# Modulating the first mixer's input in four blocks, and summing three conditioning vectors by scalings and accumulating transfers

## The chip, the core and the metric

The kernel runs on one core of a Trainium2 chip. The core has five instruction queues that run side by side and meet at semaphores: TensorE (PE, with its weight loads shown as PEld), VectorE (DVE), ScalarE (ACT), GpSimd (POOL) and SyncE (SP), which here only starts transfers. Each queue runs in order: an instruction that waits holds up all that stand behind it. The metric is the time of one execution on the device in microseconds (us); less is better.

## The reference

Two layers act on 256 tokens of 1024 features, all in float32. Each layer has a mixer and then a product-key expert block (PEER). The conditioning vector `c` gives six vectors per layer, by which the inputs are shifted and scaled and the outputs gated:

```
sh1, sc1, g1, sh2, sc2, g2 = split(silu_c @ ada_w[i] + ada_b[i], 6)
hx = x * (1 + sc1) + sh1
hc = ctx * (1 + csc1) + csh1                      # layer 0: the context too, from silu(c_ctx)
q, k, v, gu, gv = split(hx @ w_in)                # layer 0; the context gives k and v alone
a = differential attention of q over the keys and values of context and input, head norm
g = gelu(gu) * (w_s . layer_norm(gelu(gv)) + b_s)  # spatial gate
x = layer_norm(alpha * x + g1 * (concat(a, g) @ w_out))
x = layer_norm(alpha * x + g2 * peer(x * (1 + sc2) + sh2))
```

Layer 1 has a pooling mixer in place of attention. The change touches the first mixer only: how `sh1` and `sc1` of layer 0 reach `hx`, and how `g1`, `sh2` and `sc2` of layer 0 are summed.

## The kernel before

**Streaming.** All large weights come as tiles of 128 x 1024 floats (512 KB). A list of items is worked off in order: each item has a source tile and a function with its matmuls. `load` starts the transfer into `raw` (four buffers), on SP's queue, four items ahead; `split` makes of it a high part `hi` on ScalarE (line 64) and a low part `lo` = raw - hi on VectorE (line 68), three items ahead. A product of two float32 matrices is three matmuls of such parts. Every second tile of the opening uses buffers of its own (`xraw`, `xhi`, `xlo`). An item's `after` runs behind its matmuls, and `defer` puts work behind the next item's. All instructions are written out in one order per engine; nothing is moved at run time.

**Opening.** The first 16 items are the shift and scale weights, 8 tiles of 128 input rows each: for each tile, six matmuls with the two columns of `silu(c)` and `silu(c_ctx)` (`cparts`) into two accumulators, one per 512 columns. When a vector's eight tiles are done, ScalarE copies its two rows to SBUF (`adrow`, line 545), TensorE transposes them to columns (line 562), and VectorE adds the bias (line 563). Only with both vectors done does `modulated` (lines 582 to 585) make the modulated input `h` in two halves. Then the items of `w_in` begin: four tiles for `gv` (line 610, two blocks of 128 features each), four for `gu` (line 616), then four head groups of six tiles: two for the keys of input and context, two for the queries, two for the values (line 870). The context `hc` is modulated beside `gu`: ScalarE makes the high parts, GpSimd the full product (line 584), VectorE the difference.

**Head groups.** After the second key tile, `rope` copies the rotated rows on ScalarE (`rp`, line 702); VectorE multiplies and adds (lines 707 to 711) and splits the result. In the first group the exponent of lambda (line 526) and the spatial gate (`sgt`, lines 668 and 669) follow. A pipeline of scores, exponent (`ex`, line 735), transposes and value products is interleaved from there on.

**Three conditioning vectors.** `g1`, `sh2` and `sc2` of layer 0 aren't made by matmuls over `cparts`: `ada` loads eight tiles `aw` per vector, and VectorE adds tile times a column of `csil` into `aacc` (a scaling, line 391, and seven fused additions, line 393). `end` sums over the 128 partitions with matmuls by a column of ones (line 400 for a column vector, line 407 for the row vector `g1`, which goes to memory as `grow`, line 409, on ScalarE's queue). `chained` strings the vectors together; `ada_step` takes one step, and the items of a head group take 2, 2, 1, 1, 1 and 1. `aw` has three buffers, so a load waits for the addition three before it. The same `ada` serves seven vectors in layer 0's expert block.

Of the kernel before, what the change touches and what calls it, by code (L numbers as in the profile page):

```python
# [35 lines left out]
class Build:  # L36
# [335 lines left out]
            self.holds += 1  # L372


    def ada(self, pool, l, j, kind, dst, ahead=1):

        nc = self.nc
        st = {}  # L380

        def load(k):
            w = st["w", k] = pool.tile([128, 1024], FT, name="aw", bufs=3)
            nc.sync.dma_start(w, self.a["ada_w"][l, 128 * k:128 * k + 128, 1024 * j:1024 * j + 1024])

        def step(k):
            w = st.pop(("w", k))
            c = self.csil[:, k, 0:1]
            if k == 0:
                st["acc"] = pool.tile([128, 1024], FT, name="aacc", bufs=1)  # L390
                nc.vector.tensor_scalar(st["acc"], w, c, None, op0=OP.mult)
            else:
                nc.vector.scalar_tensor_tensor(st["acc"], w, c, st["acc"], op0=OP.mult, op1=OP.add)  # L393

        def end():
            acc = st["acc"]
            if kind == "col":
                p = self.pt()
                for k in range(8):
                    nc.tensor.matmul(p[:, k:k + 1], acc[:, 128 * k:128 * k + 128], self.ones[:, 0:1], start=True, stop=True)  # L400
                nc.vector.tensor_add(dst, p[:, :8], self.adabc[:, l, j])
            else:
                w = st["w", 8]
                for c in range(2):
                    s = slice(512 * c, 512 * c + 512)
                    p = self.pt()
                    nc.tensor.matmul(p[0:1], self.ones[:, 0:1], acc[:, s], start=True, stop=True)
                    nc.vector.tensor_add(w[0:1, s], p[0:1], w[0:1, s])
                nc.scalar.dma_start(dst, w[0:1])
        def go(i):  # L410
            if i < 8:
                load(i)
            elif i == 8 and kind == "row":
                w = st["w", 8] = pool.tile([128, 1024], FT, name="aw", bufs=3)
                nc.sync.dma_start(w[0:1], self.a["ada_b"][l:l + 1, 1024 * j:1024 * j + 1024])
            if i >= ahead:
                step(i - ahead)
        return [lambda i=i: go(i) for i in range(8 + ahead)], end

    @staticmethod  # L420
    def chained(vectors):

        q, end = [], None
        for steps, e in vectors:
            for i, s in enumerate(steps):
                q.append([end, s] if i == 1 and end else [s])
            end = e
        q += [[], [], [end]]
        return deque(lambda fs=fs: [f() for f in fs] for fs in q)


# [47 lines left out]
    def first(self):  # L479
# [50 lines left out]
        self.hook(start)  # L530


        for j in range(2):
            for k in range(8):
                def run(hi, lo, j=j, k=k):
                    if k == 0:
                        st["ad"] = [self.pa(), self.px()]
                    for c in range(2):
                        cs = slice(512 * c, 512 * c + 512)
                        self.mm3(st["ad"][c][0:2], (self.cparts[0][:, k], self.cparts[1][:, k]), (hi[:, cs], lo[:, cs]),  # L540
                                 k == 0, k == 7)
                    if k == 7:
                        row = st["G"].tile([2, 1024], FT, name="adrow", bufs=1)
                        for c in range(2):
                            nc.scalar.activation(row[:, 512 * c:512 * c + 512], st["ad"][c][0:2], AF.Copy)
                        if j == 0:
                            self.defer(lambda: self.defer(lambda: self.defer(lambda: columns_of(0, row))))
                        else:
                            columns_of(1, row)
                            nc.vector.tensor_scalar(st["cc"][:, 1], st["cc"][:, 1], 1.0, None, op0=OP.add)  # L550
                            self.release(1)
                            modulated(0)
                            self.ahead(self.now, 1)
                            modulated(1)
                self.item(a["ada_w"][0, 128 * k:128 * k + 128, 1024 * j:1024 * j + 1024], run,
                          after=(lambda q=k: inputs(0, [q])) if (j, k) in ((1, 0), (1, 1)) else None,
                          own=(lambda: st["E"]) if k % 2 else None, owned=2, early=k % 2)

        def columns_of(j, row):
            p = self.pt()  # L560
            for b in range(8):
                nc.tensor.transpose(p[:, 2 * b:2 * b + 2], row[:, 128 * b:128 * b + 128], self.ident[0:2, 0:2])
            nc.vector.tensor_add(st["cc"][:, j], p[:, :16].rearrange("p (k o) -> p k o", o=2),
                                 self.adabc[:, 0, j][:, :, None].to_broadcast([128, 8, 2]))


        self.holds += 1
# [5 lines left out]
        def modulated(q):  # L573
            if q == 0:
                self.hhi, self.hlo = self.htiles()
            x, y = st["in"][q], st["in"][q | 2]
            hi = self.hhi[q] if q < 2 else st["hc"][q - 2]
            lo = self.hlo[q] if q < 2 else st["hc"][q]
            for k in range(4):
                kk, o = 4 * (q % 2) + k, q // 2  # L580
                sc, sh = st["cc"][:, 1, kk, o:o + 1], st["cc"][:, 0, kk, o:o + 1]
                nc.scalar.activation(hi[:, k], x[:, k], AF.Identity, scale=sc, bias=sh)
                eng = nc.gpsimd if q else nc.vector
                eng.tensor_scalar(y[:, k], x[:, k], sc, sh, op0=OP.mult, op1=OP.add)
            nc.vector.tensor_sub(lo, y, hi.bitcast(FT))

        def others():

            P = st["P"]
            st["ada"] = self.chained([self.ada(P, 0, j, *(("row", self.growd[0][0]) if j == 2 else ("col", self.adac[:, 0, j])))  # L590
                                      for j in (2, 3, 4)])

        def ada_step(n=1):
            for _ in range(n):
                f = st["ada"] and st["ada"].popleft()
                if f:
                    f()

        def hc(k, s=slice(0, 256)):
            return st["hc"][k // 4][:, k % 4, s], st["hc"][2 + k // 4][:, k % 4, s]  # L600
# [18 lines left out]
        w = a["w_in"]  # L619
        n = 0  # L620

        for t in range(4):
            def run(hi, lo, t=t):
                if t == 0:
                    st["gv"] = [self.pa(), self.pa()]
# [2 lines left out]
                if t == 3:  # L628
# [19 lines left out]
                    def affine(nb):  # L648
# [23 lines left out]
        for t in range(4):  # L672
# [7 lines left out]
            def after(t=t):  # L680
                if t == 0:
                    small_loads("wsT", "sgu_b")
                if t == 1:
                    small_loads("lam", "ng")
                if t == 3:
                    lams()
                if t in (1, 2):
                    modulated(t + 1)
                if t == 3:
                    pe.close()  # L690
                    others()
                    st["K"] = pt_.enter_context(tc.tile_pool(name="kq", bufs=1))
            self.item(w[n], run, after=after)
            n += 1

# [20 lines left out]
        def scores(g, h, nb):  # L716
# [37 lines left out]
        def mix(g, h):  # L754
# [1 line left out]
            aT = st.pop(("aT", g, h))  # L756
            v = st["v", g]
            if h == 0:
                st["sq"] = T.tile([128, 2, 256], FT, name="sq", bufs=2)
# [139 lines left out]
        def after():  # L899
# [3 lines left out]
            if k == 8:  # L903

                assert not st["ada"]
                *st["res"], st["grow"] = [st["P"].tile([128, 1024], FT, name="aw", bufs=3) for _ in range(3)]
# [540 lines left out]
def _layout(i):  # L1447
# [5 lines left out]
    a = dict(x=g["x"][0], ada_w=g["ada_w"], ada_b=g["ada_b"], ln_g=g["ln_g"], ln_b=g["ln_b"])  # L1453
    for n, x in (("xT", "x"), ("cT", "ctx")):
        a[n] = g[x][0].T.reshape(2, 4, 128, 256).transpose(0, 2, 1, 3).reshape(2, 128, 1024)
    a["cc"] = np.stack([g["c"][0].reshape(8, 128).T, g["c_ctx"].reshape(8, 128).T], axis=2)
    a["ada_bc"] = cols(g["ada_b"].reshape(2, 6, 1024))
    a["ln_gc"], a["ln_bc"] = cols(g["ln_g"]), cols(g["ln_b"])
# [44 lines left out]
```

## Time and profile before

| | us |
|---|---|
| median of 3 runs | 2038.82 |
| lowest, highest | 2037.8, 2040.18 |
| the profiled execution, as a run | 2038.5 |
| its span, first to last instruction | 2036.7 |
| PE, DVE, ACT, POOL busy in the span | 1965.6, 1558.0, 969.6, 289.9 |

The first mixer is the first 260 us or so of the span; the opening ends at 49.50 us, and the output product of the mixer begins at 233.98 us. The profile takes one execution. A matmul's row lasts longer than the step to the next one, since matmuls overlap; the step is read from the starts. In square brackets a row names the idle time of the engine ahead of it and what ended it. Rows of DMA starts on a queue (SPq, ACTq) may last until a buffer came free.

### The profile page before, as it was taken

Reading aid. Unit: us, or ns where it says so; the run is one execution under the profiler, and the core shown is the slowest. Engines: PE = TensorE matmul, PEld = TensorE weight load, DVE = VectorE, ACT = ScalarE, POOL = GpSimd, SP = SyncE. Lnnn points to the kernel's source line nnn. Section 1 sums busy time; section 2 is a strip of 40 time slices with the busy share of each in tenths; the row PEclk is TensorE's granted clock in tenths of the full one; section 3 lists DMA queues with packets and bytes.
Section 4 is the critical chain, followed back from the end, with each engine's and each line's share of the span. In section 5 each row is a group of like instructions: output and inputs, shape, how many; then the busy total and the mean of one; then the engine's idle time right before and its main releaser. Section 6 shows DMA issues by size and latency. Waiting matters only on the chain.

```text
span 2036.7 us, 34041 instructions
## 1 busy us (share of the span) xinstructions
PE 1965.6 (97%) x13348; PEld 1771.4 (87%) x13348; DVE 1558.0 (76%) x2775; ACT 969.6 (48%) x1354; POOL 289.9 (14%) x134
## 2 busy tenths in 40 slices
PE   8899989999999999999999889999999999999997
PEld 4889869999999998888778779999999998888886
DVE  6878878998888757777776679998888655555566
ACT  6444554544544444444445554445544444444442
POOL 0100007891000000000000016890000000000001
PEclk9899999999999999999999989999999999999999
DMA  8534335554444558888877445554444556555663
GB/s 305 216 135 159 132 116 174 177 176 165 157 148 150 170 185 285 291 305 293 288 263 223 144 161 161 182 176 165 156 146 147 177 180 198 191 195 195 219 236 113
DMA packets 108178, 389.93 MB, mean 191 GB/s; under 512 B 12777, under 2 KB 12905, under 8 KB 108017
## 3 DMA queue, kind: packets, MB, share of 16 engines
q1 hardware_dynamic: 105416, 382.28, 55.8%
q10 hardware_dynamic: 2024, 3.38, 0.5%
q8 instruction: 104, 1.70, 0.3%
q0 software_dynamic: 576, 2.10, 0.3%
q14 instruction: 58, 0.47, 0.1%
HBM read 384.55 MB, written 3.16 MB: 190 GB/s over the span
## 4 chain that ended last, share of the span: by engine, by line
PE 66%; DVE 25%; ACT 4%; issue 3%; DMA 2%; ACTq 0%; SPq 0%; DVEq 0%
PE pa L323 26%; PE px L323 8%; PE pa L984 8%; PE pa L985 7%; PE pa L988 7%; PE pt L1136 2%; DVE lo L68 2%; ACT hi L64 2%; PE pa L616 1%; DVE oh L1063 1%; DVE oh L1068 1%; DVE topi L1014 1%; DVE sc L1015 1%; DVE topi L1017 1%; PE pa L870 1%
## 5 line engine op out<-in xcount | busy, mean ns | idle before, releaser
L64 ACT ACTIVATE hi<-raw 128x1024 fp32r<-128x1024 f32 x599 | 632.6, 1059 | 581.5 <-PE px L323 357.0
L68 DVE TENSOR_TENSOR lo<-raw,hi 128x1024 fp32r<-128x1024 f32 x491 | 599.5, 1224 | 368.8 <-ACT hi L64 366.8
L984 PE MATMUL pa<-h,hi 128*128 128x256 f32 x2304 | 577.9, 288 | 1.5 <-DVE h L287 1.3
L985 PE MATMUL pa<-h,hi 128*128 128x256 f32 x2304 | 566.2, 283 | 0.3
L323 PE MATMUL pa<-hi,h 128*128 128x512 f32 x1524 | 471.7, 391 | 3.3 <-ACT h L285 1.6
L984 PEld LDWEIGHTS pa<-h,hi 128*128 128x128 f32 x2304 | 441.8, 192 | 2.5 <-DVE h L287 2.1
L985 PEld LDWEIGHTS pa<-h,hi 128*128 128x128 f32 x2304 | 442.6, 192 | 0.9 <-DVE h L290 0.9
L323 PEld LDWEIGHTS pa<-hi,h 128*128 128x128 f32 x1524 | 286.3, 188 | 65.9 <-ACT h L285 1.8
L988 PE MATMUL pa<-h,lo 128*128 128x256 f32 x2304 | 323.4, 283 | 0.0
L988 PEld LDWEIGHTS pa<-h,lo 128*128 128x128 f32 x2304 | 297.7, 192 | 0.0
L68 POOL TENSOR_TENSOR lo<-raw,hi 128x1024 fp32r<-128x1024 f32 x106 | 271.0, 2575 | 81.9 <-ACT hi L64 81.6
L323 PE MATMUL pa<-lo,h 128*128 128x512 f32 x762 | 256.5, 391 | 0.1
L323 PE MATMUL px<-hi,h 128*128 128x512 f32 x508 | 197.5, 389 | 0.0
L323 PEld LDWEIGHTS pa<-lo,h 128*128 128x128 f32 x762 | 143.8, 189 | 30.6 <-DVE lo L68 0.5
L1150 ACT ACTIVATE A<-pt 128x256 f32<-128x256 f32 (+31 forms) x182 | 50.9, 310 | 229.1 <-DVE A L1148 215.9
L949 POOL DMA_DIRECT2D xhd<-xh x4 | 2.4, 596 | 960.0 <-PE pt L273 949.8
L323 PEld LDWEIGHTS px<-hi,h 128*128 128x128 f32 x508 | 95.3, 188 | 19.8
L1127 DVE TENSOR_TENSOR m<-e,gd 128x512 f16<-128x512 f16 x256 | 105.4, 454 | 2.2
L323 PE MATMUL px<-lo,h 128*128 128x512 f32 x254 | 98.8, 389 | 0.0
L259 POOL TENSOR_TENSOR aw<-aw 128x512 f32<-128x512 f32 x4 | 5.3, 1344 | 644.6 <-ACT aw L254 644.4
L393 DVE SCALAR_TENSOR_TENSOR aacc<-aw,csil,aacc 128x1024 f32<-128x1024 f32 x70 | 89.5, 1279 | 3.5 <-DMA aw<-in_ada_w 3.4
L1136 PE MATMUL pt<-m,e 128*128 128x128 f16 x1024 | 81.7, 220 | 3.2 <-DVE m L1127 1.0
(365 smaller groups left out, 2151.7 us busy)
## 6 DMA issues: line engine op xcount, KB each, us to landing
raw<-in_uT SPq DMA_DIRECT2D x256, 512.0 KB, 3.5
raw<-in_peer_v SPq DMA_DIRECT2D x256, 512.0 KB, 4.1
aw<-in_ada_w SPq DMA_DIRECT2D x80, 512.0 KB, 5.3
raw<-in_w_in SPq DMA_DIRECT2D x32, 512.0 KB, 4.1
raw<-in_wq SPq DMA_DIRECT2D x32, 512.0 KB, 3.8
raw<-in_ab_w_out SPq DMA_DIRECT2D x12, 512.0 KB, 3.5
raw<-in_ada_w SPq DMA_DIRECT2D x8, 512.0 KB, 5.9
xraw<-in_ada_w SPq DMA_DIRECT2D x8, 512.0 KB
```

The lines of the kernel that those rows point to most:

```text
L64: nc.scalar.activation(hi, it["raw"], AF.Copy)
L68: low()
L323: nc.tensor.matmul(acc[2 * nb + a // 512], s[x], w[:, a:b], start=i == 0 and part == 0, stop=i == last and part == 2)
L393: nc.vector.scalar_tensor_tensor(st["acc"], w, c, st["acc"], op0=OP.mult, op1=OP.add)
L616: nc.tensor.matmul(o, (hi, lo)[x][:, 128 * k:128 * k + 128], f(k)[y], start=k == 0 and part == 0, stop=k == 7 and part == 2)
L870: nc.tensor.matmul(p, h(k, s)[x], tiles[k // 4][y][:, 256 * (k % 4):256 * (k % 4) + 256], start=part == 0 and k == 0, stop=part == 2 and k ...
L984: mm(out, hi[:, cs], hh, start=k == 0, stop=False)
L985: mm(out, hi[:, cs], hl, start=False, stop=False)
L988: mm(out, lo[:, cs], self.h(k)[0], start=False, stop=k == 7)
L1127: nc.vector.tensor_tensor(v4(x), v4(st["e1"][:, s]), wide(st["gd"][i], ch, 4), op=OP.mult)
L1136: nc.tensor.matmul(p[:, 128 * j:128 * j + 128], e2[:, j], m[i][:, j], start=i == 0, stop=i == 1)
L1150: nc.scalar.activation(x[:, e:], y[:, e:], AF.Copy, scale=1.0 / 4096)
```

## The change

The opening goes by blocks of 256 columns: `quarter(c)` takes four tiles that hold 256 columns of shift and 256 of scale for all 1024 input rows (a new layout `ada01`), copies one row of 512 to SBUF, transposes it into four column pairs, and `modulated(c)` makes two blocks of 128 features of `h`, all on ScalarE and VectorE. The `gv` tile that reads these two blocks follows one block later: blocks 1 and 2, `w_in` tile 1, block 3, tile 2, block 4, tiles 3 and 4. The context tiles are loaded later (behind the fourth `gv` tile), and `modulated_ctx` makes both products on ScalarE.

`ada` gets a second form for the first mixer's three vectors (`dma`): ScalarE scales each tile, tiles 1 and 2 straight into two sums, the others in place; GpSimd starts a transfer that adds the scaled tile to sum 1 or 2 in turn, and after the eighth tile one that adds sum 2 to sum 1. Steps run two loads behind (`ahead=2`), `aw` has four buffers, two steps are taken before the first head group, and a vector's `end` stands two steps into the next one. To make room, the attention's `ex` buffers go from six to five and `sq` from two to one.

```diff
-    def ada(self, pool, l, j, kind, dst, ahead=1):
+    def ada(self, pool, l, j, kind, dst, ahead=1, dma=False):
...
-            w = st["w", k] = pool.tile([128, 1024], FT, name="aw", bufs=3)
+            w = st["w", k] = pool.tile([128, 1024], FT, name="aw", bufs=4 if dma else 3)
...
         def step(k):
             w = st.pop(("w", k))
             c = self.csil[:, k, 0:1]
+            if dma:
+
+                if k < 2:
+                    st["sum", k] = dma.tile([128, 1024], FT, name=f"aacc{k}", bufs=1)
+                acc = st["sum", k % 2]
+                nc.scalar.activation(w if k > 1 else acc, w, AF.Copy, scale=c)
+                if k > 1:
+                    nc.gpsimd.dma_start(acc, w, accum_op=OP.add)
+                if k == 7:
+                    nc.gpsimd.dma_start(st["sum", 0], acc, accum_op=OP.add)
+                    st["acc"] = st["sum", 0]
+                return
...
-    def chained(vectors):
+    def chained(vectors, at=1):
...
-                q.append([end, s] if i == 1 and end else [s])
+                q.append([end, s] if i == at and end else [s])
             end = e
-        q += [[], [], [end]]
+        q += [[]] * (at + 1) + [[end]]
...
-        for j in range(2):
-            for k in range(8):
-                def run(hi, lo, j=j, k=k):
...
+        def quarter(c):
+            for kk in range(4):
+                def run(hi, lo, kk=kk):
+                    if kk == 0:
+                        st["ad"] = self.px() if c % 2 else self.pa()
+                    for i in range(2):
+                        k, cs = 2 * kk + i, slice(512 * i, 512 * i + 512)
+                        self.mm3(st["ad"][0:2], (self.cparts[0][:, k], self.cparts[1][:, k]), (hi[:, cs], lo[:, cs]), k == 0, k == 7)
+                    if kk < 3:
+                        return
+                    row = st["G"].tile([2, 512], FT, name="adrow", bufs=2)
+                    nc.scalar.activation(row, st["ad"][0:2], AF.Copy)
+
+                    def turned():
+                        columns_of(c, row)
+                        modulated(c)
+                    if c == 3:
+                        self.defer(turned)
+                    else:
+                        self.defer(lambda: self.defer(turned))
...
+        def modulated(c):
...
+            for k in range(2):
+                i, kk = 2 * (c % 2) + k, 2 * c + k
+                sc, sh = st["cc"][:, 1, kk, 0:1], st["cc"][:, 0, kk, 0:1]
+                nc.scalar.activation(hi[:, i], x[:, i], AF.Identity, scale=sc, bias=sh)
+                nc.vector.tensor_scalar(y[:, k], x[:, i], sc, sh, op0=OP.mult, op1=OP.add)
+            nc.vector.tensor_sub(lo[:, ks], y, hi[:, ks].bitcast(FT))
+
+        def modulated_ctx(q):
...
+                nc.scalar.activation(hi[:, i], x[:, i], AF.Identity, scale=sc, bias=sh)
+                nc.scalar.activation(x[:, i], x[:, i], AF.Identity, scale=sc, bias=sh)
+            nc.vector.tensor_sub(lo, x, hi.bitcast(FT))
...
+            st["ada"] = self.chained([self.ada(P, 0, j, *(("row", self.growd[0][0]) if j == 2 else ("col", self.adac[:, 0, j])),
+                                               ahead=2, dma=st["K"]) for j in (2, 3, 4)], 2)
+            ada_step(2)
...
+        quarter(0)
         for t in range(4):
+            if t < 3:
+                quarter(t + 1)
+
             def run(hi, lo, t=t):
...
-            self.item(w[n], run, after=[lambda: small_loads("sgu_ln_g"), lambda: inputs(1), lambda: small_loads("sgu_ln_b"),
-                                         lambda: small_loads("rope")][t])
+            self.item(w[n], run, after=[lambda: small_loads("sgu_ln_g"), lambda: small_loads("sgu_ln_b"),
+                                         lambda: small_loads("rope"), lambda: inputs(1)][t])
...
-                x = T.tile([128, 512], FT, name="ex", bufs=6)
+                x = T.tile([128, 512], FT, name=f"ex{m}", bufs=3 - m)
```

How the opening's order moves on TensorE. Before, the last tile of the scale weights, all eight transposes of that vector and then the projections (`pa<-hi,h`), with nothing between:

```order
L156 MATMUL px<-xhi,cparts_89 2x512
L157 MATMUL px<-xlo,cparts_89 2x512
L158 MATMUL px<-xhi,cparts_90 2x512
L562 MATMUL pt<-ident,adrow 128x2 x8
L610 MATMUL pa<-hi,h 128x512 x4
L610 MATMUL pa<-lo,h 128x512 x4
L610 MATMUL pa<-hi,h 128x512 x12
```

Now, at the end of the second block, with the first projection between its last tile and its transposes:

```order
L156 MATMUL px<-xhi,cparts_89 2x512
L157 MATMUL px<-xlo,cparts_89 2x512
L158 MATMUL px<-xhi,cparts_90 2x512
L631 MATMUL pa<-hi,h 128x512 x4
L631 MATMUL pa<-lo,h 128x512 x4
L631 MATMUL pa<-hi,h 128x512 x4
L572 MATMUL pt<-ident,adrow 128x2 x4
L156 MATMUL pa<-hi,cparts_89 2x512
```

Twelve projections of the first `gv` tile have moved in front of the third block's tiles, and the transposes are four at a time.

ScalarE's queue in the second head group, from the split before the gate row's transfer (`grow`) on. Before:

```order
L64 ACTIVATE hi<-raw 128x1024
L409 DMA grow_102<-aw 1x1024
L702 ACTIVATE rp<-pa 32x512 x4
L161 ACTIVATE kT_1224<-pa 128x2x256
L161 ACTIVATE aT_1237<-pt 128x4x128
L735 ACTIVATE ex,asum<-pt,amx 128x512
L735 ACTIVATE ex,amx<-pt,amx 128x512
L64 ACTIVATE hi<-raw 128x1024 x2
```

Now, with the first two scalings of the second vector (into its two sums, `aacc_1248` and `aacc_1252`) and two of its scalings in place:

```order
L422 DMA grow_102<-aw 1x1024
L394 ACTIVATE aacc_1248<-aw,csil 128x1024
L394 ACTIVATE aacc_1252<-aw,csil 128x1024
L727 ACTIVATE rp<-pa 32x512 x4
L161 ACTIVATE kT_1254<-pa 128x2x256
L161 ACTIVATE aT_1267<-pt 128x4x128
L760 ACTIVATE ex_1286,asum<-pt,amx 128x512
L760 ACTIVATE ex_1289,amx<-pt,amx 128x512
L64 ACTIVATE hi<-raw 128x1024
L394 ACTIVATE aw<-aw,csil 128x1024
L64 ACTIVATE hi<-raw 128x1024
L394 ACTIVATE aw<-aw,csil 128x1024
```

Two scalings stand between the transfer and the rotation's copies, and one between the two splits.

## Rows read from the trace of the kernel before

**Rows 1.** Stretches: busy us of each engine (count), granted clock, DMA share, GB/s.

```profile
80.00:100.00 20.00, 12.40 (x84) 11.91 (x83) 19.55 (x29) 4.01 (x6) 0.00 (x0) 0.74 0.53 193
```

**Rows 2.** TensorE's waits from 60 to 120 us: total us, times, longest.

```profile
PE pa L870 <- DVE lo L68: 7.6, 2, 4.0
```

**Rows 3.** Timeline of the opening: start us, us, engine, line, operation, tiles, [idle before].

```profile
5.31 1.06 ACT L64 ACTIVATE hi<-raw 128x1024 fp32r<-128x1024 f32 x1 [2.68 <-DMA raw<-in_ada_w]
...
12.30 1.06 ACT L64 ACTIVATE xhi<-xraw 128x1024 fp32r<-128x1024 f32 x1 [0.41 <-DMA xraw<-in_ada_w]
...
14.66 0.40 PE L156 MATMUL pa<-hi,cparts 128*2 128x512 f32 x1
...
16.05 0.40 PE L156 MATMUL pa<-xhi,cparts 128*2 128x512 f32 x1
...
31.67 0.59 ACT L545 ACTIVATE adrow<-pa 2x512 f32<-2x512 f32 x1 [3.81 <-PE pa L158]
...
32.31 0.41 PE L562 MATMUL pt<-ident,adrow 2*128 2x2 f32 x4
...
34.50 1.53 PE L610 MATMUL pa<-hi,h 128*128 128x512 f32 x4 [1.11 <-ACT h L582]
...
43.14 1.08 PE L610 MATMUL pa<-lo,h 128*128 128x512 f32 x4
...
49.50 2.08 PE L616 MATMUL pa<-h,hi 128*128 128x256 f32 x16
...
56.33 2.08 ACT L582 ACTIVATE hc<-in,mod 128x256 fp32r<-128x256 f32 x4 [0.28 <-issue]
```

**Rows 4.** Timeline of TensorE at the third group's value tiles.

```profile
176.74 0.74 PE L870 MATMUL pa<-lo,h 128*128 128x256 f32 x4 [1.26 <-DVE lo L68]
...
180.22 2.96 PE L870 MATMUL pa<-hi,h 128*128 128x256 f32 x16
```

**Rows 5.** VectorE's groups, 60 to 240 us: count, busy us, mean ns, idle before.

```profile
L393 DVE SCALAR_TENSOR_TENSOR aacc<-aw,csil,aacc 128x1024 f32<-128x1024 f32 x21 | 26.9, 1280 | 3.5 <-DMA aw<-in_ada_w 3.4
```

**Rows 6.** The chain that ended last, 60 to 80 us: start, us, what.

```profile
73.11 5.92 DMA aw<-in_ada_w
```

**Rows 7.** Timeline of the first head group.

```profile
67.81 0.90 SPq L384 DMA_DIRECT2D aw<-in_ada_w  x2
...
70.93 2.40 ACT L702 ACTIVATE rp<-pa 32x512 f32<-32x512 f32 x4 [2.77 <-PE pa L616]
...
75.72 0.20 ACT L526 ACTIVATE sl<-sl 128x2 f32<-128x2 f32 x1
...
79.14 1.28 DVE L393 SCALAR_TENSOR_TENSOR aacc<-aw,csil,aacc 128x1024 f32<-128x1024 f32 x1 [3.43 <-DMA aw<-in_ada_w]
...
81.79 0.68 DVE L668 TENSOR_TENSOR sgt<-pt,sgu_b 128x512 f32<-128x512 f32 x1
...
83.23 0.43 DVE L200 CAST cat<-sgt 128x512 fp32r<-128x512 f32 x1
...
91.66 1.22 DVE L68 TENSOR_TENSOR lo<-raw,hi 128x1024 fp32r<-128x1024 f32 x1
```

**Rows 8.** Timeline of the second head group.

```profile
120.68 2.39 ACT L702 ACTIVATE rp<-pa 32x512 f32<-32x512 f32 x4 [7.83 <-DVE aw L408]
...
128.10 0.74 PE L870 MATMUL pa<-hi,h 128*128 128x256 f32 x4 [1.26 <-ACT hi L64]
...
134.44 1.22 PE L870 MATMUL pa<-lo,h 128*128 128x256 f32 x4 [3.21 <-DVE lo L68]
```

**Rows 9.** Timeline of the fourth head group.

```profile
203.93 2.40 ACT L702 ACTIVATE rp<-pa 32x512 f32<-32x512 f32 x4
...
209.62 0.68 DVE L162 TENSOR_TENSOR kT<-pa,kT 128x512 fp32r<-128x512 f32 x1
```

**Rows 10.** GpSimd's plain transfers: issue ns min/median/max, and time to landing in us.

```profile
L949 POOL DMA_DIRECT2D xhd<-xh x4: 533/559/733, 287.3 to 1202.8; - x4
...
DMA to landing us min/median/max: 2.9/3.0/8.6
```

More of the change, by code (lines that the diff above doesn't have):

```diff
@@ L413, in go @@
             elif i == 8 and kind == "row":
-                w = st["w", 8] = pool.tile([128, 1024], FT, name="aw", bufs=3)
+                w = st["w", 8] = pool.tile([128, 1024], FT, name="aw", bufs=4 if dma else 3)
                 nc.sync.dma_start(w[0:1], self.a["ada_b"][l:l + 1, 1024 * j:1024 * j + 1024])
@@ L530, in first @@
         self.hook(start)
-        for j in range(2):
-            for k in range(8):
-                def run(hi, lo, j=j, k=k):
[L536 to L557, printed above, removed]
@@ L559, in columns_of @@
-        def columns_of(j, row):
+        def quarter(c):
[17 more added lines that the diff above has]
+                        self.defer(lambda: self.defer(turned))
+                self.item(a["ada01"][c, kk], run, after=(lambda: inputs(0, [c])) if kk == 1 and c < 2 else None,
+                          own=(lambda: st["E"]) if kk % 2 else None, owned=2, early=kk % 2)
@@ L560, in columns_of @@
+        def columns_of(c, row):
             p = self.pt()
-            for b in range(8):
+            for b in range(4):
                 nc.tensor.transpose(p[:, 2 * b:2 * b + 2], row[:, 128 * b:128 * b + 128], self.ident[0:2, 0:2])
-            nc.vector.tensor_add(st["cc"][:, j], p[:, :16].rearrange("p (k o) -> p k o", o=2),
-                                 self.adabc[:, 0, j][:, :, None].to_broadcast([128, 8, 2]))
-        self.holds += 1
+            ks = slice(2 * c, 2 * c + 2)
+            for j in range(2):
+                nc.vector.tensor_add(st["cc"][:, j, ks], p[:, 4 * j:4 * j + 4].rearrange("p (k o) -> p k o", o=2),
+                                     self.adabc[:, 0, j, ks][:, :, None].to_broadcast([128, 2, 2]))
+            nc.vector.tensor_scalar(st["cc"][:, 1, ks], st["cc"][:, 1, ks], 1.0, None, op0=OP.add)
@@ L571, in inputs @@
                 nc.sync.dma_start(st["in"][2 * o + q].rearrange("p k n -> p (k n)"), a["cT" if o else "xT"][q])
-        def modulated(q):
-            if q == 0:
+        def modulated(c):
+            if c == 0:
                 self.hhi, self.hlo = self.htiles()
[L576 to L591, printed above, removed]
+            q, ks = c // 2, slice(2 * (c % 2), 2 * (c % 2) + 2)
+            x, hi, lo = st["in"][q], self.hhi[q], self.hlo[q]
+            y = st["G"].tile([128, 2, 256], FT, name="xmod", bufs=1)
+            for k in range(2):
[5 more added lines that the diff above has]
+        def modulated_ctx(q):
+            x, hi, lo = st["in"][2 + q], st["hc"][q], st["hc"][2 + q]
+            for i in range(4):
+                kk = 4 * q + i
+                sc, sh = st["cc"][:, 1, kk, 1:2], st["cc"][:, 0, kk, 1:2]
+                nc.scalar.activation(hi[:, i], x[:, i], AF.Identity, scale=sc, bias=sh)
+                nc.scalar.activation(x[:, i], x[:, i], AF.Identity, scale=sc, bias=sh)
+            nc.vector.tensor_sub(lo, x, hi.bitcast(FT))
         def ada_step(n=1):
@@ L597, in ada_step, with others @@
                     f()
+        def others():
+            P = st["P"]
+            st["ada"] = self.chained([self.ada(P, 0, j, *(("row", self.growd[0][0]) if j == 2 else ("col", self.adac[:, 0, j])),
+                                               ahead=2, dma=st["K"]) for j in (2, 3, 4)], 2)
+            ada_step(2)
         def hc(k, s=slice(0, 256)):
@@ L687, in after @@
                 if t in (1, 2):
-                    modulated(t + 1)
+                    modulated_ctx(t - 1)
                 if t == 3:
                     pe.close()
+                    st["K"] = pt_.enter_context(tc.tile_pool(name="kq", bufs=1))
                     others()
-                    st["K"] = pt_.enter_context(tc.tile_pool(name="kq", bufs=1))
             self.item(w[n], run, after=after)
@@ L758, in mix @@
             if h == 0:
-                st["sq"] = T.tile([128, 2, 256], FT, name="sq", bufs=2)
+                st["sq"] = T.tile([128, 2, 256], FT, name="sq", bufs=1)
                 st["og"] = T.tile([128, 2, 256], FT, name="og", bufs=2)
@@ L905, in after @@
                 assert not st["ada"]
-                *st["res"], st["grow"] = [st["P"].tile([128, 1024], FT, name="aw", bufs=3) for _ in range(3)]
+                *st["res"], st["grow"] = [st["P"].tile([128, 1024], FT, name="aw", bufs=4) for _ in range(3)]
                 for i in range(2):
@@ L1455, in _layout @@
         a[n] = g[x][0].T.reshape(2, 4, 128, 256).transpose(0, 2, 1, 3).reshape(2, 128, 1024)
+    a["ada01"] = g["ada_w"][0][:, :2048].reshape(4, 2, 128, 2, 4, 256).transpose(4, 0, 2, 1, 3, 5).reshape(4, 4, 128, 1024)
     a["cc"] = np.stack([g["c"][0].reshape(8, 128).T, g["c_ctx"].reshape(8, 128).T], axis=2)
```

1 line of the change is left out of this document (added).

## The prediction

> **What bounds the kernel now.** I read the stretches first. Between 80 and 100 us TensorE is busy for 12.40 of 20 us, VectorE for 19.55, and the granted clock is 0.74 [rows 1]: part of that stretch runs at the lower level of 1.2 GHz. The waits of TensorE then name the work: in 60 to 120 us it waits 7.6 us in two waits for `lo` tiles that VectorE subtracts [rows 2]. Such waits are where the second part of the change can pay; where TensorE doesn't wait, what VectorE sheds is worth nothing. Third, the timeline of the opening [rows 3]: tiles of the conditioning weights come every 1.40 us ((12.30 − 5.31) / 5) and cost TensorE 1.39 us each (16.05 − 14.66), so both run level, and the sixteen tiles cannot be hurried. What is open is the seam: from 32.31 to 34.50 us TensorE does transposes and waits, and then its first projections run at 1.53 us for four where 1.08 is the later price. The first `w_in` projection ends where the next phase starts, at 49.50 us.
>
> **First part: modulation in four blocks.** No tile is added or removed, and 48 projections of 512 columns stay. I walk the new order with row durations; six matmuls in 1.39 us make 0.23 us each. The first five tiles are as before (to 16.05); transposes of block 1 take 0.4, three tiles 4.2: 20.7. The first projection's tile is now the tenth transfer, so it comes at 5.31 + 9 × 1.40 = 17.9. ScalarE must first split the tile ahead of it (1.06 each: 20.0), VectorE subtracts (1.22: 21.2) and only then, by its order, makes the columns (three small additions, 0.5 by estimate), and ScalarE the modulated block (0.52 each, from the four of 2.08 at 56.33): about 22.0. TensorE waits 1.3, then projects 12 × 0.23 = 2.8: 24.8. ScalarE meanwhile splits three tiles (3.2) before it copies row 2 (0.59): 25.8. So TensorE waits 1.0 more, transposes 0.4, then four tiles, a projection, transposes and four tiles (5.6 + 2.8 + 0.4 + 5.6): 40.7. Row 4 has nothing in front of its chain: 1.4 of waiting, 0.4 of transposes, and two projections of 2.8 give 48.0. That is 1.5 us before 49.50, at full clock.
>
> But three pauses of 1.3 to 1.8 us, with nothing but transposes in them, replace one of 2.2. After the one of 2.2 the projections ran slow [rows 3]; after one of 1.26 in the third head group a block that takes 2.08 at full clock took 2.96 [rows 4]. If the clock falls once, at the last pause, 24 projections at +0.11 ((1.53 − 1.08) / 4) cost 2.7. I halve this chance: 1.5 − 1.4, about 0. Bounds: +1.5 with no fall, −6.6 with three.
>
> **Second part: three vectors on ScalarE and in transfers.** VectorE loses 21 additions of 1.28 us [rows 5] and three scalings. ScalarE gains 24 scalings; a pass of its over the same shape is 1.06 [rows 3], two are 2.1. GpSimd's queue gains 21 transfers of 512 KB. The context's modulation leaves GpSimd for ScalarE: twice 2.08 more there [rows 3]. What matters is that ScalarE's queue is in order too, and that the scalings stand in front of the copies of the rotation (`rp`), from which the keys, the attention scores and the next splits follow. Group by group, in times of the old trace:
>
> Group 1. Before, VectorE waited 3.43 us for a weight tile (asked for at 73.11, 5.92 us on its way [rows 6]) and added from 79.14; its gating work began at 81.79 and the second `lo` of the value tiles came at 91.66 + 1.22 [rows 7]. Now ScalarE waits for the same tiles. The first pair has one `w_in` transfer fewer before it and is there in time. The second pair takes the first pair's old place, 67.81, made some 1.2 later by ScalarE's longer modulation: about 69. With 5.92 us it is there at 75.0, and one pace later at 76.4; the scalings end at 77.5. Only then come `rp`, the key copy and the exponent, which took from 70.93 to 75.92, 4.5 without a short wait for TensorE in them: 82.0. VectorE's gating work stands behind an operation on that exponent and starts at 82.3, 0.5 later than before, though VectorE is idle. Then one addition of 1.28 less stands before the second `lo`: gain 0.8, and with the earlier relief I take 1.0. Bounds: 0, and 4.7 if the pair is there in time (the scalings then end 3.9 sooner, and with them all that follows: 0.8 + 3.9).
>
> Group 2. ScalarE is held at 120.68 by the transfer of the gate row, 7.83 us [rows 8]; the two scalings of the next vector now follow it and push `rp` by 2.1. Another scaling comes between the two splits that TensorE waits for. The first split (TensorE at 128.10, 1.26 waited) is 2.1 later; the second `lo` gains 1.28 and a little and loses 2.1 and more: 135.5 for 134.44. Loss 1.1; bounds −3.2 (2.1 and 1.06, nothing won back) and +1.28.
>
> Group 3. The closing matmuls of vector 2 go behind the first query tile, and nothing stands before `rp` that was not there. The stall of 1.26 goes, and the slow stretch after it: 0.9 on the block of 2.96 [rows 4], and some 0.6 by estimate on the scores between: +2.8. Bounds +1.3 and +2.8.
>
> Group 4. Four scalings, 4.2 us, now stand around the split before `rp`, which begins at 203.93 before [rows 9]. Its end goes from 206.3 to 210.5; the key's `lo` (209.62) needs it and comes at about 211.2. TensorE has little slack there: −1.5; bounds −3 and 0.
>
> The transfers. None is shown. The last two of a vector are a chain (eighth tile into sum 2, then sum 2 into sum 1), and TensorE's closing matmuls, and ScalarE's scaling that rewrites sum 1, wait for its end. For vector 1 the eighth scaling ends near 105.2 and the matmuls are due at 116.0: 10.8 us for two, of which 0.56 each is issue [rows 10]; for vector 2 it is 158.8 and 168.0, or 9.2 (estimates: the old times of the work around them, moved by the terms above). So the point is 4.0 to 4.8 us per transfer. A plain one of this size on that queue landed in 2.9 to 8.6, median 3.0 [rows 10]. With the destination read too I take one more pace, 3.0 + 1.4 = 4.4: loss 0.8 at vector 2. Bounds: 0 at 3.0, and at 8.6 about 7.5 + 9.1 = 16.6. The Trainium skill prices a transfer on this path as 2.0 us plus bytes over 436 GB/s (DMA: Bandwidth & Descriptors, Anatomy of one DMA), 3.2 us here, which agrees with the median of 3.0; by it the loss of 0.8 goes and the sum is 0.8 better. Another page speaks against the change: GpSimd writes these descriptors into SBUF, and a VectorE instruction in a two-port mode shuts it out (SBUF — State Buffer, Who interferes with whom); no run here shows it yet. VectorE's copies in this phase take 0.43 us [rows 7]; one in front of each of the two issues would make 0.8 into 1.7.
>
> Sum: 0 + 1.0 − 1.1 + 2.8 − 0.8 − 1.5 = 0.4 us gained. Against the profiled execution (2038.5, of which the span is 2036.7; it is 0.3 under the median of the runs) that is 2038.1; I say 2038.
>
> **Rivals.**
> *ScalarE's waits are covered (faster).* For: ScalarE is busy only 4.01 of 20 us where VectorE is full [rows 1]. Against: the 5.92 us of the weight tile. Then group 1 gives 4.7, and about 0.9 of clock as in group 3 (an estimate), groups 2 and 4 nothing, group 3 2.8, the opening 1.5: 9.9, so 2028.6.
> *The transfer chain becomes TensorE's wait (slower).* Place: the closing matmuls after vectors 1 and 2. Decides from about 4.6 us each. At 8.6, the slowest of the nearest row, 16.6 less the 1.2 otherwise won: 2053.9; at 6 us, 2.3 + 3.9 = 6.2, so 2043.5. For: an addition needs the destination as well, and the queue is shared with the weight stream. Against: 3.0 median.
> *The clock falls at each pause of the opening (slower).* 3 × 2.7 − 1.5 = 6.6 lost: 2045.1. For: what followed the pauses in [rows 3, 4]; against: the new ones are shorter than 2.2.
>
> **How the numbers follow.** Forecast (relief and new waits cancel) 0.39, its own range 2034.5 to 2042.5. ScalarE covered 0.36. Transfer chain 0.15. Clock 0.10. A measurement of this kernel tells 0.2%, 4.1 us, from no change; so faster 0.36, same 0.39, slower 0.25. The range of eight in ten leaves out the far end of the transfers and the last of the first rival: 2029 to 2046.
>
> **What would show it.** Opening: the first matmul of the second projection phase near 48 us, with three pauses before it and the clock level in them. Group 1: ScalarE idle before its third scaling for a weight tile; if it does not wait, the first rival holds. Group 2: `rp` 2 us behind the gate row's transfer. Group 3: no wait of 1.26. Transfers: their time to landing, and whether TensorE waits before the closing matmuls. A wait longer than 2 us there, or a time under 2033, would make the prediction wrong.

## The result, and the profile after

The changed kernel takes 2053.12 us (median of 4 runs, 2052.34 to 2057.48) for 2038.31 of the kernel before on the same chip: ratio 1.0076, interval 1.0064 to 1.0088. It is slower by some 15 us, where no change was forecast, and above the forecast range.

First the stretches of the changed kernel (columns as in [rows 1]):

```profile
20.00:40.00 20.00, 18.84 (x88) 9.31 (x86) 17.92 (x27) 16.06 (x21) 0.00 (x0) 1.00 0.88 323
...
80.00:100.00 20.00, 15.16 (x109) 14.18 (x109) 14.91 (x23) 8.50 (x15) 2.57 (x3) 0.91 0.96 256
100.00:120.00 20.00, 14.36 (x101) 11.65 (x100) 6.98 (x10) 5.42 (x9) 1.71 (x2) 0.87 0.68 185
...
160.00:180.00 20.00, 10.69 (x87) 9.94 (x85) 9.95 (x16) 9.14 (x16) 2.59 (x3) 0.82 0.91 252
```

Between 80 and 100 us what was meant to get better did: TensorE is busy for 15.16 us where it was 12.40, VectorE for 14.91 where it was 19.55, and the clock is higher [rows 1]. But from 160 to 180 us TensorE has only 10.69 us of work, and nobody else is busy either: VectorE, ScalarE and GpSimd are all under half. Only the DMA engines are (0.91), at a rate of 252 GB/s. That is the picture of a wait for transfers. TensorE's timeline in the changed kernel, around the two stretches, names them:

```profile
110.94 1.12 PE L637 MATMUL pa<-hc,lo 128*128 128x256 f32 x8
117.70 3.57 PE L420 MATMUL pt<-aacc,ones 128*1 128x512 f32 x4 [5.64 <-DMA aacc<-aacc]
...
169.57 1.12 PE L637 MATMUL pa<-h,lo 128*128 128x256 f32 x8
180.53 3.55 PE L413 MATMUL pt<-ones,aacc 128*128 128x1 f32 x16 [9.84 <-DMA aacc<-aacc]
183.94 3.76 PE L637 MATMUL pa<-h,hi 128*128 128x256 f32 x16
187.50 1.91 PE L637 MATMUL pa<-h,lo 128*128 128x256 f32 x8
189.21 2.30 PE L895 MATMUL pa<-hi,h 128*128 128x256 f32 x16
```

The closing matmuls of vectors 1 and 2 wait 5.64 and 9.84 us for the last transfer of the chain, sum 2 into sum 1. Behind each wait the clock is at its lower level of 1.2 GHz for a while: the 16 projections at 183.94 take 3.76 us where 2.08 is their price at full clock [rows 3]. GpSimd's queue shows the links (a start waits for the transfer whose sum it needs):

```profile
101.43 0.86 POOL L396 DMA_DIRECT2D aacc<-aw  x1 [10.36 <-ACT aw L394]
106.78 0.86 POOL L398 DMA_DIRECT2D aacc<-aacc  x1 [4.50 <-DMA aacc<-aw]
...
161.90 0.86 POOL L396 DMA_DIRECT2D aacc<-aw  x1 [0.18 <-issue]
172.18 0.86 POOL L398 DMA_DIRECT2D aacc<-aacc  x1 [9.42 <-DMA aacc<-aw]
```

From start to start and from the last start to TensorE, the links took 5.35 and 10.92 us for vector 1, 10.28 and 8.35 for vector 2. All 21, in the view of the sums on GpSimd's queue alone:

```profile
DMA to landing us min/median/max: 4.5/7.6/11.6
```

ScalarE pays for the first wait as well. It starts the gate row's transfer from its own queue and can do nothing until the closing matmuls and VectorE's addition are done; the two scalings then stand in front of `rp`, as in the forecast, but the hold is 15.13 us where it was 7.83 [rows 8]:

```profile
122.63 2.19 ACT L394 ACTIVATE aacc<-aw,csil 128x1024 f32<-128x1024 f32 x2 [15.13 <-DVE aw L421]
124.84 2.39 ACT L727 ACTIVATE rp<-pa 32x512 f32<-32x512 f32 x4
```

The opening is better than walked. TensorE's timeline of the changed kernel:

```profile
20.94 1.09 PE L631 MATMUL pa<-hi,h 128*128 128x512 f32 x4
...
24.32 0.40 PE L572 MATMUL pt<-ident,adrow 2*128 2x2 f32 x4 [0.48 <-ACT adrow L557]
...
39.85 0.41 PE L572 MATMUL pt<-ident,adrow 2*128 2x2 f32 x4 [0.68 <-ACT adrow L557]
...
45.76 2.08 PE L637 MATMUL pa<-h,hi 128*128 128x256 f32 x16
```

The pauses are 0.48 and 0.68 us before transposes and none before the first projections, the clock stays at 1.00, and the second phase begins at 45.76 where it was 49.50 [rows 3]. By the second late `lo` of the first head group TensorE is 5.26 us ahead: it starts on it at 87.67, where it was 92.93 (in [rows 7] VectorE's subtraction ends at 92.88). So the first wait for the chain is met with a lead of some 5.4 us (112.06, where TensorE was ready at 117.5 before), and still the mixer's end is late: its output product starts at 252.42 for 233.98, 18.4 us. The profiled spans differ by 14.5 only. Of the 3.9 us between, 1.7 come back within the output product, where waits of 1.04 and 0.28 us for VectorE are gone; the rest comes later and was not followed.

### The profile page after: what moved, and what is told of

Same layout as the page of the kernel before. It is cut to its first block, busy times and chain, and to the rows that moved or that the text cites. A ratio compares the mean times of both kernels' runs of the same rounds, so it can differ in the third digit from the quotient of the medians.

```text
span 2051.2 us, 34136 instructions
## 1 busy us (share of the span) xinstructions
PE 1970.0 (96%) x13348; PEld 1776.2 (87%) x13348; DVE 1533.1 (75%) x2766; ACT 1000.0 (49%) x1386; POOL 298.6 (15%) x143
## 3 DMA queue, kind: packets, MB, share of 16 engines
q0 software_dynamic: 3600, 13.11, 3.1%
## 4 chain that ended last, share of the span: by engine, by line
PE 64%; DVE 22%; DMA 5%; ACT 5%; issue 3%; ACTq 0%; SPq 0%; POOL 0%; DVEq 0%; POOLq 0%
PE pa L323 26%; PE px L323 8%; PE pa L1009 8%; PE pa L1013 7%; PE pa L1010 7%; PE pt L1161 2%; DVE lo L68 2%; ACT hi L64 2%; DVE oh L1088 1%; DVE oh L1093 1%; DMA aacc<-aw 1%; DVE topi L1039 1%; DVE sc L1040 1%; DVE topi L1042 1%; PE pa L895 1%
## 5 line engine op out<-in xcount | busy, mean ns | idle before, releaser
L162 DVE TENSOR_TENSOR h<-A,h 128x1024 fp32r<-128x1024 f32 (+1 forms) x66 | 78.8, 1194 | 1.4 <-ACT h L161 1.4
```

The costliest lines, as they stand in the source:

```text
L162: self.nc.vector.tensor_sub(lo, src, hi.bitcast(FT))
```

## The experiments

Ratios are to the kernel before on the same chip, with their interval; "us" is a median. Several kernels leave something out, and their "Expected" says what. The theories: A, TensorE waits for the chain of transfers, and that is the whole loss; B, VectorE bounds the first head group; C, the load of the transfers on the weight stream is the loss; D, ScalarE, held by the gate row, makes the waits of the second group.

**The parts apart.** `e1_blocks_alone`, from the changed kernel:

```diff
-                                               ahead=2, dma=st["K"]) for j in (2, 3, 4)], 2)
-            ada_step(2)
+                                               ) for j in (2, 3, 4)])
```

Expected: 

> The modulation in four blocks and the context on ScalarE as in the changed kernel; the three vectors summed by VectorE as in the kernel before (three aw buffers, one load ahead, six ex and two sq buffers). Theory A, the opening is worth what its timeline shows and all of the loss comes from the transfers: the second projection phase begins 3.7 us earlier (45.76 for 49.50), about 2034.5 us in all, ratio 0.998. Theory B, VectorE is the bound of the first head group and takes the lead back: about 2038, ratio 1.000. If the blocks themselves cost something behind the opening: over 2039.

Measured 2036.28 us, ratio 0.9989 (0.9980 to 0.9998). `e2_sums_alone` is the kernel before with the new `ada` and its buffers:

```diff
-                                      for j in (2, 3, 4)])
+                                               ahead=2, dma=st["K"]) for j in (2, 3, 4)], 2)
+            ada_step(2)
```

Expected: 

> The opening of the kernel before, with the three vectors scaled on ScalarE and summed by accumulating transfers on two sums, as in the changed kernel. Theory A (all of the loss is here): 2053 plus the 3.7 us of the opening, 2056 to 2057 us, ratio 1.009. If the loss needs both parts (the context's modulation on ScalarE in front of the scalings): about 2045.

Measured 2057.00 us, ratio 1.0092 (1.0076 to 1.0107), with the same two waits (5.6 and 7.8 us). So all of the loss comes with the sums. The blocks gain 2.2 us (0.4 to 4.1). Their second phase starts 3.4 earlier (46.09), but in the trace only 1.55 of that is left at the second late `lo` of the first group, which VectorE starts at 90.11 where it was 91.66 [rows 7]: theory B holds in part. The interval of the medians would allow the whole 3.4. The row in `e1_blocks_alone`:

```profile
90.11 1.22 DVE L68 TENSOR_TENSOR lo<-raw,hi 128x1024 fp32r<-128x1024 f32 x1
```

**Is it the wait, or the load on the DMA engines?** Two kernels tell that apart. `e8_no_transfers`:

```diff
-                if k > 1:
-                    nc.gpsimd.dma_start(acc, w, accum_op=OP.add)
                 if k == 7:
-                    nc.gpsimd.dma_start(st["sum", 0], acc, accum_op=OP.add)
```

Expected: 

> The changed kernel with all 21 transfers left out, so that the vectors hold only the first two tiles' products; the scalings on ScalarE stay. It prices what is left of the change without any transfer. By the prediction's terms for the head groups (1.0 - 1.1 + 2.8 - 1.5 = 1.2 gained) behind the blocks alone (2036.3): 2035 us. Theory A, the transfers' wait is the whole loss: 2033 to 2037. Rival, ScalarE's queue in order (held 15.1 us at 122.63) costs as much: over 2040.

Measured 2033.02 us, ratio 0.9972 (0.9963 to 0.9982): without transfers the change is a gain. `e9_nobody_waits` keeps all of them:

```diff
-                acc = st["sum", k % 2]
-                nc.scalar.activation(w if k > 1 else acc, w, AF.Copy, scale=c)
+                acc = self.aside[k % 2]
+                nc.scalar.activation(w, w, AF.Copy, scale=c)
...
-                    st["acc"] = st["sum", 0]
+                    st["acc"] = self.hhi[0].rearrange("p a b -> p (a b)").bitcast(FT)
```

Expected: 

> The changed kernel with all 21 accumulating transfers, but into two tiles that nobody reads; the closing matmuls read another tile, so the vectors are not the sums. The first two tiles are scaled in place. It splits the 20 us between the changed kernel (2053.1) and the one without transfers (2033.0). Theory A, waiting for the chain is the loss: 2033 to 2037 us, though the transfers load the DMA engines as before. Theory C, the load that they put on the weight stream is the loss: 2045 us or more. In between, the split of the two.

Measured 2032.59 us, ratio 0.9970 (0.9958 to 0.9983). Its page and its stretches:

```profile
q0 software_dynamic: 3600, 13.11, 3.1%
```

```profile
160.00:180.00 20.00, 20.00 (x166) 19.03 (x165) 15.43 (x31) 12.31 (x19) 1.82 (x2) 1.00 0.94 280
```

GpSimd's queue moves the same 13.11 MB, and the DMA engines are as busy from 160 to 180 us as in the changed kernel (0.94 for 0.91); but TensorE works all 20 us at full clock. The load by itself costs TensorE nothing that can be measured; the waiting costs all. The sum nearly closes: in `e9_nobody_waits` the closing matmuls take

```profile
113.57 1.88 PE L424 MATMUL pt<-h,ones 128*1 128x512 f32 x4
...
165.53 1.84 PE L417 MATMUL pt<-ones,h 128*128 128x1 f32 x16
```

so the changed kernel's two waits (5.64 + 9.84) and what runs at the lower clock behind them (3.57 − 1.88, 3.55 − 1.84 and 3.76 − 2.08: 5.1) make 20.6 us; the two rows after that, at 187.50 and 189.21, add 1.0 (1.12 and 2.08 at full clock). The medians differ by 20.5 us, the profiled spans by 21.0. ScalarE's hold at the gate row is back at 7.70 us too, and TensorE's waits for `hi` behind it are as long as in the changed kernel (4.8 us for 4.2), so the longer hold is no part of the loss that can be seen.

**What makes the chain long.** `e4_plain_copies`:

```diff
-                    nc.gpsimd.dma_start(acc, w, accum_op=OP.add)
+                    nc.gpsimd.dma_start(acc, w)
...
-                    nc.gpsimd.dma_start(st["sum", 0], acc, accum_op=OP.add)
+                    nc.gpsimd.dma_start(st["sum", 0], acc)
```

Expected: 

> The changed kernel with the same 21 transfers as plain copies into the sums, without adding, so that the three vectors hold only the last tiles' products. Theory A1, the addition is the price: landing falls from a median of 7.4 us to about 3 to 4 us, the two waits go, 2031 to 2036 us. Theory A2, the path (SBUF to SBUF from GpSimd's queue beside the weight stream) is the price: landing stays over 6 us and the time over 2048 us.

Measured 2040.30 us (2035.26 to 2041.82), ratio 0.9999 (0.9990 to 1.0009): between the two. The view of the sums on GpSimd's queue:

```profile
L396 POOL DMA_DIRECT2D aacc<-aw x18: 527/527/725, 72.0 to 211.7; - x18
...
DMA to landing us min/median/max: 2.8/5.5/9.8
```

and its page's row for the queue:

```profile
q0 software_dynamic: 3600, 13.11, 1.6%
```

The addition takes 2.0 us or so of each landing (4.5, 7.6 and 11.6 for 2.8, 5.5 and 9.8), 0.33 us of each start (0.86 for 0.53), and doubles the time on the DMA engines: 21 transfers took some 57 us of them (3.1% of 2051.2, less the 0.3% of 2036.7 before), plain ones 26 (1.6% of 2039.3, less the same). TensorE's waits fall to 2.6 and 1.2 us but don't go. So both theories hold in part: a plain transfer beside the weight stream isn't 3 us either. How much the stream does, the same trace shows. For the eighth tile of vector 1 and the link behind it I took the DMA view over just the time each was on its way, 102.33 to 105.23 us and 105.75 to 115.55 (packets, MB, share of the 16 engines; q0 is GpSimd's queue, q1 carries the weights):

```profile
q0 software_dynamic: 144, 0.52, 44.5%
q1 hardware_dynamic: 1, 0.00, 0.8%
...
q1 hardware_dynamic: 693, 2.52, 75.8%
q0 software_dynamic: 144, 0.52, 13.3%
```

The same plain 512 KB took 2.9 us where next to no weights moved, and 9.8 us beside 2.52 MB of them. In the changed kernel these two took 4.8 us beside 0.17 MB and 10.9 us beside 2.22 MB. The eighth tile of vector 2 took 9.7 us beside 1.67 MB, and shared its queue with the seventh, which had started only 1.04 us before it; the link behind it took 8.2 us beside 1.06 MB. So the addition makes some 2 us of a landing, and the traffic beside it up to 7.

`e3_no_last_link` drops one of the two links:

```diff
-                if k == 7:
-                    nc.gpsimd.dma_start(st["sum", 0], acc, accum_op=OP.add)
-                    st["acc"] = st["sum", 0]
+                st["acc"] = [st["sum", i] for i in range(min(k + 1, 2))]
...
+                    for i, x in enumerate(accs):
+                        nc.tensor.matmul(p[:, k:k + 1], x[:, 128 * k:128 * k + 128], self.ones[:, 0:1], start=i == 0, stop=i == len(accs) - 1)
```

Expected: 

> The changed kernel without the transfer that adds sum 2 to sum 1: the closing matmuls take both sums, twice as many, accumulated in PSUM. Theory A, the chain of transfers sets the end of a vector and TensorE waits for it: the last link took 10.9, 8.2 and 5.5 us by its windows, so the waits of 5.6 us after vector 1 and 9.8 us after vector 2 fall to 0 and about 1, the slow clock behind them goes (some 8 us in both), less 1.9 us for the added matmuls: 2031 to 2037 us. Theory C, the waits only stand where the loss shows and its root is the weight stream, held up by the accumulating transfers: the wait moves on to later tiles, and less than 6 us come back, 2047 us or more.

Measured 2044.49 us (2038.51 to 2049.70), ratio 1.0034 (1.0022 to 1.0047): 8.6 us of the loss come back, less than theory A asked. In the profiled execution, the fastest, the waits are gone but for 0.95 us, and the doubled closing matmuls take 5.4 us more, about what it lies above the 2033.0 without transfers:

```profile
113.47 3.59 PE L422 MATMUL pt<-aacc,ones 128*1 128x512 f32 x8
...
166.06 0.28 PE L413 MATMUL pt<-ones,aacc 128*128 128x1 f32 x2
167.29 3.51 PE L413 MATMUL pt<-ones,aacc 128*128 128x1 f32 x30 [0.95 <-DMA aacc<-aw]
```

1.7 us more for vector 1, 1.9 for vector 2 and 1.8 for vector 3 (3.63 at 234.16). Why its other runs, at a granted clock of 0.982 to 0.985 where this one has 0.989, are 4 to 11 us longer stays open: the one trace doesn't show it.

`e11_no_link_gate_queue` adds to it that the gate row is started from GpSimd's queue:

```diff
-                nc.scalar.dma_start(dst, w[0:1])
+                (nc.gpsimd if dma else nc.scalar).dma_start(dst, w[0:1])
```

Expected: 

> The changed kernel without the last link (both sums in the closing matmuls), and the gate row started from GpSimd's queue. Theory D, ScalarE's 15.1 us behind the gate row's transfer make the hi waits of the second head group (4.3 us): 2038 to 2041 for the 2044.5 without. Rival, the scalings in front of rp make them: 2044.

Measured 2042.77 us, ratio 1.0015 (1.0006 to 1.0024). TensorE's waits for `hi` in the second group fall from 4.3 to 2.6 us, and one of 0.97 for `lo` comes: theory D, in part. The medians differ by 1.7 us, on two chips, with intervals that overlap at their ends.

**Better versions.** With the sums back on VectorE. `e5_first_vector_gpsimd`, from the blocks alone:

```diff
+            if late and kind == "row":
+                nc.gpsimd.tensor_scalar(w if k else st["acc"], w, c, None, op0=OP.mult)
+                if k:
+                    nc.gpsimd.tensor_add(st["acc"], st["acc"], w)
```

Expected: 

> The blocks alone, and the first of the three vectors summed on GpSimd (a scaling and an addition for each tile) in place of VectorE; no transfers. Theory B, VectorE bounds the first head group (18.21 of 20 us busy between 80 and 100 us, TensorE waits 8.0 us for lo): the waits shrink by what VectorE sheds there (five additions of 1.28 and a wait of 3.88 for a weight tile), some 5 us gained over the blocks alone: 2030 to 2033 us, ratio 0.996. Rival, GpSimd is too slow for a tile every 5 us (its 128x256 passes took 0.55 to 1.1 us, so two passes of 128x1024 are 4.4 to 8.8 us) and the closing matmuls wait for it: 2040 us or more.

Measured 2037.12 us, ratio 0.9992 (0.9983 to 1.0001). The time lies between the two, but the rival's wait is there: a scaling took 2.9 to 4.9 us on GpSimd, an addition 2.3 to 3.1, and the closing matmuls wait for them, with the lower clock behind:

```profile
119.37 3.57 PE L424 MATMUL pt<-aacc,ones 128*1 128x512 f32 x4 [4.22 <-POOL aacc L406]
```

`e6_gate_row_queue` is the blocks alone with one other line:

```diff
-                nc.scalar.dma_start(dst, w[0:1])
+                (nc.gpsimd if late else nc.scalar).dma_start(dst, w[0:1])
```

Expected: 

> The blocks alone, and the transfer of the gate row started from GpSimd's queue, not from ScalarE's. Theory D, ScalarE is held by that transfer (7.83 us idle at 119.79, the copies rp behind it) and this makes TensorE's waits of the second group (4.7 us for lo, 1.5 for hi): these go, 2031 to 2034 us. Rival, VectorE is late there by itself: 2036, as the blocks alone.

Measured 2034.39 us, ratio 0.9975 (0.9966 to 0.9984): the lowest median of those that compute the reference. ScalarE copies the rotation in the second group six us earlier than in the blocks alone, where the row stood at 119.79:

```profile
113.67 2.39 ACT L726 ACTIVATE rp<-pa 32x512 f32<-32x512 f32 x4 [1.90 <-PE pa L636]
```

TensorE's first wait for `hi` there (1.25 us) goes; the wait of 3.2 for VectorE's `lo` stays. `e7_gpsimd_and_queue` has both edits (those of e5 and e6). Expected: 

> Both: first vector on GpSimd, gate row from GpSimd's queue. If each takes its own wait away the gains add: 2026 to 2030 us. If one takes what the other had: no better than the better of the two.

Measured 2034.45 us (2033.89 to 2039.87; three of eleven runs are 2 to 5 us above the median), ratio 0.9987 (0.9978 to 0.9997): no better than the better of the two. `e10_blocks_more_ahead`, from e6:

```diff
-                                               late=True) for j in (2, 3, 4)])
+                                               ahead=2, late=st["K"]) for j in (2, 3, 4)], 2)
+            ada_step(2)
```

Expected: 

> The blocks alone with the gate row on GpSimd's queue, and the additions still on VectorE, but with the changed kernel's fourth aw buffer, loads two steps ahead and two steps taken before the first head group (five ex and one sq buffer to make room). If VectorE's wait for a weight tile in the first head group (3.88 us in the blocks alone) is passed on to TensorE: it goes, and 2030 to 2032 us. Rival, the tile wait only moves VectorE's additions, which still stand before the lo: 2034, as without.

Measured 2035.08 us, ratio 0.9981 (0.9972 to 0.9990), no better than e6. The first group's second `lo` is used 2.6 us earlier (89.09 for 91.69), but in the fourth group TensorE waits 2.0 us for `lo`, where it was 0.9, and 1.4 for `hi`, where it was nothing: given back.

## Why the prediction was wrong

*The step that failed* is the term "With the destination read too I take one more pace, 3.0 + 1.4 = 4.4: loss 0.8 at vector 2". The mechanism of the chain, its places and its allowances were right. The eighth scaling of vector 1 ended at 101.13 and TensorE was ready at 112.06: 10.9 us (10.8 were worked out); for vector 2, 161.60 to 170.69: 9.1 (9.2). What was mis-sized is the transfer: its landing took 4.8, 10.9, 9.7 and 8.2 us in the two chains, not 4.4, which is the price of the quickest of the 21 (4.5). It was taken from four plain transfers that had the DMA engines nearly to themselves (in the 4 us from 287 on, around the first of them, all queues together moved 131 GB/s, which is that one transfer). The chain runs where weights are on their way, not on one queue with them, as the rival has it, but over the same 16 engines; in the stretch with vector 1's last link the changed kernel's transfers took, in the view of DMA issues from 100 to 112 us (KB each, median us to landing),

```profile
aw<-in_ada_w SPq DMA_DIRECT2D x3, 512.0 KB, 11.5
raw<-in_w_in SPq DMA_DIRECT2D x2, 512.0 KB, 9.7
aacc<-aw POOLq DMA_DIRECT2D x1, 512.0 KB, 4.8
aacc<-aacc POOLq DMA_DIRECT2D x1, 512.0 KB, 10.9
```

So the second rival held, and nearly at its upper price: 16.6 us of waiting at 8.6 per transfer, where 15.5 were measured. That its time came so near, 2053.9 for 2053.1, is luck, for two errors met there. The clock behind the waits (5.1 us) was not in the rival; and what the rest of the change gains was 5.7 us (below), not 1.2. The 8.6 itself was misread: in [rows 10] the landing counts every queue's transfers of that tile; on GpSimd's queue alone the kernel before has

```profile
DMA to landing us min/median/max: 2.9/2.9/3.1
```

The forecast's range ended at 2046 and left out the far end of its own bound, though no row excluded it.

*Opening*: forecast 0, with bounds of +1.5 and −6.6; measured +3.7, outside them. What failed is the length of the pauses: 1.3, 1.0 and 1.4 were walked, and 0.48 and 0.68 us stand there, 2.5 us less. Without a long pause the clock didn't fall, so the third rival is out: what the seam before had cost in clock came back too.

*Group 1*: forecast +1.0. ScalarE does wait for its third scaling, 1.99 us, as was said; the second `lo` comes 5.26 us earlier, of which 3.7 are the opening's: +1.5. *Group 2*, read in `e9_nobody_waits`, where the chain doesn't cover it: `rp` does stand 2.2 us behind the hold, TensorE waits 3.53 and 1.24 us, both for `hi`, in place of 1.26 for `hi` and 3.21 for `lo` [rows 8]: 0.3 more, and what follows runs at the lower clock (0.83 from 120 to 140 us). *Group 3*: the wait of 1.26 [rows 4] is gone there, with 20.00 busy at clock 1.00. *Group 4*: a wait of 2.01 for `lo` came, for the forecast 1.5. In `e8_no_transfers` these terms and the opening give 5.7 us (3.7 to 7.5) of gain; the forecast for them was 1.2.

*The first rival* (ScalarE covered, 2028.6) was out: ScalarE waits. `e8_no_transfers` comes within 5 us of it, which is what the change could have been worth with a free sum.

*The rules of the Trainium skill.* By DMA: Bandwidth & Descriptors (Anatomy of one DMA) a link takes 3.2 us, an estimate. For accumulating transfers the measured 4.5 to 11.6 decide against it; plain ones come near it where next to no weights moved (2.9), not beside them (up to 9.8). The rule that a two-port mode of VectorE shuts GpSimd out from writing descriptors (SBUF — State Buffer, Who interferes with whom) was not put to the test: the forecast's condition, a copy of VectorE in front of the chain's starts, didn't come. At the four starts VectorE was idle (101.43, 161.90) or in a pass of 0.27 us on one column (106.79) or a multiplication of two tiles (172.17), and each took 0.86 us.

## What to carry to other kernels

A transfer in a chain that an engine waits for is priced under the load of its place: count what else moves on the DMA engines while it is on its way. The slowest that the trace shows there, once per transfer of the chain, is the upper end (21.8 us here, where the two chains took 16.3 and 18.6), and a transfer in a quiet stretch is the lower end. If a wait is possible, count the clock behind it: here a third was added to each microsecond of waiting. And look at what else stands on the queue that starts a transfer: moving one small start from ScalarE's queue to an idle one took a wait of 1.25 us from TensorE, and the median was 1.9 us lower (2034.39 for 2036.28; on two chips, with intervals that overlap by a little, so the size is not sure).

## What was not expected of the hardware

An accumulating transfer of 512 KB from SBUF to SBUF keeps the DMA engines about twice as long as a plain one (57 us for 21, against 26), and its start takes GpSimd 0.86 us against 0.53. Its load slowed TensorE by nothing that can be measured where nothing waited for it (2032.59 us with all 21, 2033.02 with none), though the median landing of the `w_in` tiles was 3.6 us with none and 6.8 with all from 60 to 240 us; items are loaded four ahead. What the load does lengthen is the transfers themselves, from 2.9 to 9.8 us for the same plain 512 KB.
